# Matmuls of ones around the first transposes, and GpSimd in written order, at the beginning of a two-layer encoder kernel

## The chip, the cores and the metric

The kernel runs on one core of a Trainium2 chip. The metric is the device time of one execution in microseconds (us), shown as the median of several runs. The core has five engines with instruction queues of their own, which wait for each other through semaphores: TensorE (PE; its weight loads are shown apart as PEld), VectorE (DVE), ScalarE (ACT), GpSimd (POOL) and SyncE (SP), which here only issues DMAs. Matmuls write to PSUM, the accumulation memory; the other operands lie in SBUF.

## The reference

Two interleaved layers over 1024 tokens of width 1024, float32. Each layer is `x = x + mixer(rms_norm(x))`, then `x = x + ffn(rms_norm(x))`; a last `rms_norm` ends it.

- Layer 0 mixes with differential attention: 8 heads, each with two query/key pairs of 64, of which 16 are rotated by position, and values of 128. The weights of one softmax minus lambda times those of the other multiply the values; the result is normalised per head and projected.
- Layer 1 mixes with latent attention: 16 heads whose queries, keys and values come out of normalised low-rank projections (ranks 384 and 256) and a rotated key shared by the heads.
- The feed-forward part projects to 2 x 2816, applies a causal convolution of width 3, a gated SiLU, and projects back.

Attention is causal in chunks of 64 tokens.

## The kernel before, in words

Every float32 product is made of three matmuls in the faster type fp32r: an operand is split into a rounded part ("high", a cast, L127) and the rest ("low", a subtraction, L130). `mm3` (L119 to L121) issues the three. So each operand is transposed where needed, cast, and subtracted before PE can use it.

The change lies in `diff_attention`, at the beginning of layer 0. There the 1024 tokens come in as eight tiles `x` of 128 tokens. For each tile ACT sums the squares (`squares`, L157), DVE and POOL make the root (L164 and L167, a power), DVE normalises (`norm`, L370), PE transposes the tile in two groups of four 128x128 blocks (`turn`, L378), ACT casts the high half of each group (`high`) and DVE subtracts the low half (`parts_low`, `low`). The first head's three weight tensors (`which` 0 queries, 1 keys, 2 values) are split likewise (`w_high`, `w_low`). `piece(which, part)` then issues 24 matmuls, 256 tokens wide, that make a quarter of the tokens of one projection; `complete` rotates the result (`rope`: DVE L237 and L238, POOL L239 and L240) and splits it again (L574, L575 for keys; casts L127 on ACT and subtractions L130 on POOL for queries; a copy L560 for values, which are transposed later at L186).

Three things set the order of the work. From `region.__enter__()` to `region.__exit__()` the engines named there follow the order in which the code is written: PE, DVE and ACT. All else is placed by a planner that simulates the program and chooses which instruction each engine issues next; it also places every instruction after the region. Each queue is then executed in that order. POOL and SP are the planner's from the start.

After the region, `steps` runs the attention of head after head, four steps each. `prepare` fetches and splits the next head's weights (`fetch_w`, `split_w`: a cast on ACT, a subtraction on POOL); `units` issues the next projections, `scores` the query-key products (L1553 and L1554 in the first attention, mm3 into tiles named S in the second), `weigh`, `turn` and `product` what follows. The scores lie in two PSUM buffers named S; projections use one buffer named u, transposes and others three named b. The second attention, of layer 1, has the same kind of steps (exponential L1637, products with the values L1657 and L1658), all placed by the planner.

`ones` is a 128x128 tile of ones in fp32r (L208), made from the identity `ident`. `h4` is a piece of SBUF which the first attention uses only late in each head (`R.fin`).

Of the kernel before, what the change touches and what calls it, by code (L numbers as in the profile page):

```python
# [11 lines left out]
F32R = mybir.dt.float32r  # L12
AF = mybir.ActivationFunctionType
ALU = mybir.AluOpType
# [4 lines left out]
P = 128  # L19
# [7 lines left out]
DA_HEADS = 8  # L27
# [29 lines left out]
class Trunk:  # L57
# [123 lines left out]
    def turn_blocks(self, src, dst):  # L181
# [6 lines left out]
        self.hi(dst(0), v)  # L188
        self.lo(dst(1), v, dst(0))

    def gain(self, place, src):
        g = self.at(place, [P, src.shape[-1]])
        self.nc.sync.dma_start(g, src.partition_broadcast(P))
        return g


    def constants(self):
        nc, a = self.nc, self.a
        c = lambda name, shape, dt=F32: self.const.tile(shape, dt, name=name, tag=name)
        self.ident = c("ident", [P, P])  # L200
        make_identity(nc, self.ident)
        nc.scalar.preload_act_table_set("natural_log_exp_and_others")
        self.mhalf = c("mhalf", [P, 1])
        nc.gpsimd.memset(self.mhalf, -0.5)
        self.eps = c("eps", [P, 1])
        nc.gpsimd.memset(self.eps, EPS)
        self.ones = c("ones", [P, P], F32R)
        nc.vector.tensor_scalar(self.ones, self.ident, 0.0, 1.0, ALU.mult, ALU.add)  # L208
        self.conv = [c(f"conv{l}", [P, 2 * NF, 4]) for l in range(2)]
        self.g_sub = c("g_sub", [P, 1])  # L210
        self.neglam = c("neglam", [P, 1])
# [103 lines left out]
    def diff_attention(self, o_d, prefetch):  # L315
        nc, a = self.nc, self.a
# [7 lines left out]
            P=self.ring("u8", "u9", "u10", "u11", "u12"), pT=self.ring("u13", "u14", "u15"),  # L324
# [9 lines left out]
        raws = {}  # L334

        def fetch_w(h, which):
            if h < DA_HEADS:
                raws[h, which] = self.fetch(a["da_wqkv"][h, which], D)

        def split_w(h, which):  # L340
            if h < DA_HEADS:
                raw = raws.pop((h, which))
                w = self.w([P, 2, D], F32R)
                self.hi(w[:, 0, :], raw)
                self.lo(w[:, 1, :], raw, w[:, 0, :], nc.gpsimd)
                heads[h]["w", which] = w[:, 0, :], w[:, 1, :]

        def unit(h, which, half):
# [9 lines left out]
        def fetch_x(i):  # L358
            x.append(R.P([P, D]))
            nc.sync.dma_start(x[i], a["x"][i * P : (i + 1) * P, :])  # L360
# [5 lines left out]
        def squares(i):  # L366
            r[i] = self.squares(x[i], junk)
# [4 lines left out]
        def root(i):  # L372
            r[i] = self.root(r[i], D)

        def turn(i, kg):
            ps = part_of[i, kg] = self.bank()
            for k in range(4):
                nc.tensor.transpose(ps[:, k * P : (k + 1) * P], x[i][:, (4 * kg + k) * P : (4 * kg + k + 1) * P], self.ident)  # L378

        def parts(i, kg):  # L380
            s = slice((i % 4) * P, (i % 4 + 1) * P)
            return part_of[i, kg].rearrange("p (k s) -> p k s", s=P), [H[part][i // 4][kg][:, :, s] for part in range(2)]

        def high(i):
            for kg in range(2):
                src, (hi, lo) = parts(i, kg)
                self.hi(hi, src)
# [10 lines left out]
        def w_high(which):  # L398
            raw = raws[0, which]
            w = heads[0]["wt", which] = self.w([P, 2, D], F32R)  # L400
            heads[0]["w", which] = w[:, 0, :], w[:, 1, :]
            self.hi(w[:, 0, :], raw)

        def w_low(which):
            w = heads[0]["wt", which]
            self.lo(w[:, 1, :], raws.pop((0, which)), w[:, 0, :])
# [13 lines left out]
        def complete(which):  # L420
            return self.da_complete(R, accs[which], which, 0, heads[0], tab)

        def turns(i):
            for kg in range(2):
                turn(i, kg)
# [9 lines left out]
        nc.sync.dma_start(raws[0, 2], a["da_wqkv"][0, 2])  # L435
        fetch_tab(0)
        fetch_x(4)
        region = self.tc.manual_schedule(engines={mybir.EngineType.PE, mybir.EngineType.DVE, mybir.EngineType.Activation})
        region.__enter__()
        one, two = range(0, 4), range(4, 8)  # L440
        squares(0)
        root(0)
        norm(0)
        squares(1)
        root(1)
        turns(0)
        high(0)
        w_high(1)
        parts_low(0, 0)
# [1 line left out]
        parts_low(0, 1)  # L451
        squares(2)
        turns(1)
        high(1)
        w_low(1)
        root(2)
# [47 lines left out]
        queries, value = [complete(0)], [complete(2)]  # L504
# [8 lines left out]
        self.run(queries)  # L513
        fetch_w(1, 1)
        self.load_constants()
        region.__exit__(None, None, None)
        self.run(value)

        def prepare(t):
            h, p = divmod(t, 4)  # L520
            if p == 0:
                split_w(h + 1, 1)
                fetch_w(h + 1, 0)
            if p == 1:
                split_w(h + 1, 0)
                fetch_w(h + 1, 2)
            if p == 2:
                split_w(h + 1, 2)
            if p == 3:
                fetch_w(h + 2, 1)  # L530
            if h + 1 == DA_HEADS:
                prefetch()
# [732 lines left out]
    def mla_input(self, W, hts, turns, v_d, heads_of):  # L1265
# [28 lines left out]
        def latents(i):  # L1294
            acc = self.big()
            for k in range(KD):
                for b, m, kind in ((0, 384, "q"), (512, 288, "kv")):
                    wh, wl = where[kind, k]
                    self.mm3(acc[:, b : b + m], hts[i][:, 0, k, :], hts[i][:, 1, k, :], wh, wl, k == 0, k == KD - 1)
            nat = nats([P, 672])  # L1300
            for b, m, off, gain in ((0, 384, 0, g[0]), (512, 256, 384, g[1])):
                d = nat[:, off : off + m]
                r = self.rstd(acc[:, b : b + m], d, m)
                nc.vector.scalar_tensor_tensor(d, acc[:, b : b + m], r, gain, ALU.mult, ALU.mult)
            nc.scalar.copy(nat[:, 640:672], acc[:, 768:800])
            return nat
# [646 lines left out]
```

## Time and profile before

| what | us |
|---|---|
| median of 3 runs | 2432.36 (2431.1 to 2434.21) |
| the profiled execution | 2430.82 |
| its span, from first to last instruction | 2429.0 |
| TensorE busy | 2361.7 (97%) |
| DVE / ACT / POOL busy | 1899.3 / 1304.4 / 625.3 |

The page's rows of an engine's timeline show start and length in us, engine, line, what was done, output and input tile (buffer numbers left out) with their shapes, and in brackets how long the engine was idle before it and who ended that. A table of stretches shows, for each stretch of time, its length, then the busy time of PE, PEld, DVE, ACT and POOL with the number of instructions, the clock that TensorE was granted (1.00 is full), the share of the DMA engines, and GB/s. A row of waits shows who waited for whom, the total in us, how often, and the longest. Matmuls overlap each other, so their spacing, not their length, tells the rate.

### The profile page before, as it was taken

The numbers are of one execution on the slowest core, as the hardware profiler recorded it, in microseconds if no ns is written. First come the engines' busy times: TensorE is split into PE (matmuls) and PEld (weight loads), VectorE is DVE, ScalarE is ACT, GpSimd is POOL, SyncE is SP. The second block draws the span as 40 slices with busy tenths as digits, with TensorE's granted clock in tenths as the row PEclk, the third lists the DMA queues.
The fourth block names the chain that finished last, engine by engine and source line by source line (L and its number), as shares of the span: only waits on it lengthen the run. The fifth ranks groups of instructions, "written<-read, shape, count | busy, mean of one in ns | idle before, by whom it ended". The sixth has DMA issues, their size and how long they took to land. (4 is left out here: it accounts for less than half of the span.)

```text
span 2429.0 us, 32810 instructions
## 1 busy us (share of the span) xinstructions
PE 2361.7 (97%) x12032; PEld 2007.0 (83%) x12032; DVE 1899.3 (78%) x3094; ACT 1304.4 (54%) x2434; POOL 625.3 (26%) x500
## 2 busy tenths in 40 slices
PE   7999999999999999999999999999999999999998
PEld 6888878788888888878898788988888888887886
DVE  6677777756888888899964788886478888888997
ACT  5677776844444444444445777775344444444444
POOL 4545555425000000000042666664330000000001
PEclk9999999999999999999999999999999999999999
DMA  4111111333222222553221211123322222227502
GB/s 161 47 37 36 35 36 44 100 100 126 70 78 83 83 80 93 194 175 120 84 90 55 68 40 40 40 76 119 108 70 87 78 88 86 78 87 277 171 3 79
DMA packets 95793, 213.93 MB, mean 88 GB/s; under 512 B 8720, under 2 KB 33936, under 8 KB 95632
## 3 DMA queue, kind: packets, MB, share of 16 engines
q1 hardware_dynamic: 86448, 184.04, 22.9%
q10 hardware_dynamic: 9184, 27.79, 3.1%
q8 instruction: 95, 1.56, 0.3%
q14 instruction: 66, 0.54, 0.1%
HBM read 159.37 MB, written 52.43 MB: 87 GB/s over the span
## 5 line engine op out<-in xcount | busy, mean ns | idle before, releaser
L167 POOL TENSOR_TENSOR st<-st,mhalf 128x1 f32<-128x1 f32 x56 | 35.7, 638 | 1311.7 <-DVE st L164 1306.7
L127 ACT CAST u<-h 128x512 fp32r<-128x512 f32 (+2 forms) x242 | 146.1, 619 | 280.2 <-DVE h L779 260.1
L119 PE MATMUL S<-s,u 128*128 128x512 f32 (+1 forms) x752 | 286.0, 380 | 0.7 <-DVE s L130 0.5
L120 PE MATMUL S<-s,u 128*128 128x512 f32 (+1 forms) x752 | 284.6, 379 | 0.0
L121 PE MATMUL S<-s,u 128*128 128x512 f32 (+1 forms) x752 | 284.6, 378 | 0.0
L119 PE MATMUL b<-s,u 128*128 128x512 f32 x588 | 230.8, 392 | 2.1 <-DVE S L1635 1.0
L121 PE MATMUL b<-s,u 128*128 128x512 f32 x588 | 229.2, 390 | 0.0
L120 PE MATMUL b<-s,u 128*128 128x512 f32 x588 | 229.2, 390 | 0.0
L836 DVE SCALAR_TENSOR_TENSOR u<-u,conv,u 128x1023 f32<-128x1023 f32 (+1 forms) x176 | 224.7, 1277 | 1.6 <-ACT u L832 1.6
L149 POOL TENSOR_TENSOR u<-u,st 128x384 f32<-128x384 f32 (+7 forms) x160 | 169.2, 1067 | 151.4 <-DVE st L1643 107.8
L127 ACT CAST s<-u 128x512 fp32r<-128x512 f32 (+2 forms) x202 | 128.8, 673 | 110.4 <-PE u L121 35.9
L119 PE MATMUL u<-s,s 128*128 128x512 f32 (+1 forms) x440 | 176.7, 402 | 11.1 <-DVE h L238 4.5
L130 DVE TENSOR_TENSOR u<-b,u 128x512 fp32r<-128x512 f32 (+1 forms) x256 | 157.7, 629 | 24.3 <-ACT u L127 22.4
L121 PE MATMUL u<-s,s 128*128 128x512 f32 (+1 forms) x440 | 172.9, 393 | 0.0
L120 PE MATMUL u<-s,s 128*128 128x512 f32 (+1 forms) x440 | 172.2, 391 | 0.0
L119 PEld LDWEIGHTS S<-s,u 128*128 128x128 f32 x752 | 141.8, 189 | 27.9 <-DVE s L130 0.9
L121 PEld LDWEIGHTS S<-s,u 128*128 128x128 f32 x752 | 141.9, 189 | 26.2
L120 PEld LDWEIGHTS S<-s,u 128*128 128x128 f32 x752 | 141.9, 189 | 26.0
L127 ACT CAST u<-b 128x512 fp32r<-128x512 f32 (+1 forms) x256 | 133.5, 549 | 28.1 <-PE b L252 22.3
L839 ACT ACTIVATE u<-u 128x1024 f32<-128x1024 f32 x44 | 46.8, 1062 | 187.5 <-DVE u L836 187.5
L130 DVE TENSOR_TENSOR s<-u,s 128x512 fp32r<-128x512 f32 (+2 forms) x187 | 127.4, 714 | 17.7 <-ACT s L127 17.6
L130 DVE TENSOR_TENSOR u<-h,u 128x512 fp32r<-128x512 f32 x166 | 114.1, 687 | 32.4 <-ACT u L127 31.5
(263 smaller groups left out, 6632.1 us busy)
## 6 DMA issues: line engine op xcount, KB each, us to landing
u<-in_ffn_up SPq DMA_DIRECT2D x88, 512.0 KB, 3.9
g_d<-u ACTq DMA_DIRECT2D x44, 512.0 KB, 2.6
u<-in_ffn_down SPq DMA_DIRECT2D x66, 256.0 KB, 4.7
u<-g_d SPq DMA_DIRECT2D x62, 256.0 KB, 4.3
s<-in_da_wqkv SPq DMA_DIRECT2D x23, 512.0 KB, 3.3
x_d<-u SPq DMA_DIRECT2D x16, 512.0 KB, 3.0
s<-x_d SPq DMA_DIRECT2D x8, 1024.0 KB, 10.5
u<-o_d SPq DMA_DIRECT2D x24, 256.0 KB, 2.9
```

Of the source, the lines that this page charges most:

```text
L119: mm(out, lh, rl, start=first, stop=False, skip_group_check=onto)
L120: mm(out, lh, rh, start=False, stop=False, skip_group_check=onto)
L121: mm(out, ll, rh, start=False, stop=last, skip_group_check=onto)
L127: self.nc.scalar.copy(out, src)
L130: (eng or self.nc.vector).tensor_sub(out, src, hi.bitcast(F32))
L149: self.nc.gpsimd.tensor_mul(x, x, s.to_broadcast(list(x.shape)))
L167: nc.gpsimd.tensor_tensor(r, s, self.mhalf, ALU.pow)
L836: nc.vector.scalar_tensor_tensor(t[half][:, back:], u[half][:, : S - back], w, t[half][:, back:], ALU.mult, ALU.add)
L839: nc.scalar.activation(t[0], t[0], AF.Silu)
```

## The change

- A method `spin(n)` issues `n` matmuls of the ones tile with a 512-wide tile of ones into the u buffer. Nobody reads the results; the first piece writes the same buffer afterwards. `spin(14)` stands ahead of everything in the region, `spin(3)` after the first tile's transposes, `spin(1)` after the second tile's.
- The wide tile of ones is made by four DVE writes out of `ident`, in `h4`.
- POOL is added to the engines whose order in the region is the written one.
- The value's completion (`self.run(value)`) moves into the region, and the second head's key weights (1, 1) are split there, at its end, with the subtraction on DVE; `prepare` skips them then, since `raws` no longer has them.

```diff
+    def spin(self, n):
+        ps = self.bank("u")
+        for _ in range(n):
+            self.nc.tensor.matmul(ps, self.ones, self.wide, start=True, stop=True)
...
+        self.wide = self.at("h4", [P, 512], F32R)
+        for j in range(4):
+            nc.vector.tensor_scalar(self.wide[:, j * P : (j + 1) * P], self.ident, 0.0, 1.0, ALU.mult, ALU.add)
...
-        def split_w(h, which):
-            if h < DA_HEADS:
+        def split_w(h, which, eng=None):
+            if (h, which) in raws:
...
-                self.lo(w[:, 1, :], raw, w[:, 0, :], nc.gpsimd)
+                self.lo(w[:, 1, :], raw, w[:, 0, :], eng or nc.gpsimd)
...
-        region = self.tc.manual_schedule(engines={mybir.EngineType.PE, mybir.EngineType.DVE, mybir.EngineType.Activation})
+        region = self.tc.manual_schedule(engines={mybir.EngineType.PE, mybir.EngineType.DVE, mybir.EngineType.Activation, mybir.EngineType.Pool})
...
+        self.spin(14)
         squares(0)
...
         turns(0)
+        self.spin(3)
         high(0)
...
         turns(1)
+        self.spin(1)
         high(1)
...
         fetch_w(1, 1)
         self.load_constants()
+        self.run(value)
+        split_w(1, 1, nc.vector)
         region.__exit__(None, None, None)
-        self.run(value)
```

As built, each engine has the same instructions as before but for the 18 matmuls, the four writes and the subtraction that goes from POOL to DVE. Their order is the same outside the beginning, save in the second attention, where the planner places PE's, DVE's, ACT's and POOL's instructions differently.

## The prediction

> **What bounds the kernel now.** I read the page's totals first, then a table of stretches, then the timeline of each engine over the first 66 us, then PE's waits.
>
> ```profile
> span 2429.0 us, 32810 instructions
> PE 2361.7 (97%) x12032; PEld 2007.0 (83%) x12032; DVE 1899.3 (78%) x3094; ACT 1304.4 (54%) x2434; POOL 625.3 (26%) x500
> ...
> 14.20:19.40 5.20, 5.15 (x24) 5.15 (x25) 4.45 (x5) 2.12 (x4) 1.46 (x1) 1.00 0.91 334
> 36.40:51.30 14.90, 11.10 (x64) 8.95 (x62) 11.78 (x21) 7.98 (x14) 12.18 (x8) 1.00 0.11 37
> 75.00:105.00 30.00, 30.00 (x153) 25.07 (x152) 18.50 (x33) 19.44 (x37) 12.79 (x10) 1.00 0.05 18
> ```
>
> TensorE is busy 97% of the span. From 75 to 105 us it never rests, so whatever the beginning saves or loses ahead of that arrives at the end unless a later stall takes it up. Two stretches of the beginning are slow in different ways. From 14.2 to 19.4 us PE is full (5.15 of 5.20) with only 24 matmuls; from 36.4 to 51.3 it idles 3.8 of 14.9 us. The profiled execution took 2430.82 us, 1.8 more than its span; the median of the runs, 2432.36, is 1.5 above it. The sums below are made on the profiled one, and their difference is put on the median.
>
> ```profile
> 1.98 0.52 DVE L208 TENSOR_SCALAR ones<-ident 128x128 fp32r<-128x128 f32 x1 [1.98 <-POOL ident masks.py:199]
> 5.79 0.15 DVE L164 TENSOR_SCALAR st<-st 128x1 f32<-128x1 f32 x1 [3.29 <-ACT u L157]
> 8.03 1.97 PE L378 MATMUL b<-ident,u 128*128 128x128 f32 x8 [8.03 <-DVE u L370]
> 9.18 0.59 ACT L127 CAST s<-b 128x512 fp32r<-128x512 f32 x1 [0.20 <-PE b L378]
> 9.80 0.69 DVE L130 TENSOR_TENSOR s<-b,s 128x512 fp32r<-128x512 f32 x1 [0.63 <-ACT s L127]
> 11.73 1.97 PE L378 MATMUL b<-ident,u 128*128 128x128 f32 x8 [1.74 <-DVE u L370]
> 12.20 1.21 DVE L130 TENSOR_TENSOR s<-s,s 128x1024 fp32r<-128x1024 f32 x1
> 14.25 0.58 PE L119 MATMUL u<-s,s 128*128 128x256 f32 x1 [0.55 <-DVE s L130]
> 14.63 0.42 PE L120 MATMUL u<-s,s 128*128 128x256 f32 x1
> 19.11 0.42 PE L120 MATMUL u<-s,s 128*128 128x256 f32 x1
> 19.52 1.04 PE L378 MATMUL b<-ident,u 128*128 128x128 f32 x8
> 20.52 0.28 PE L120 MATMUL S<-s,s 128*128 128x256 f32 x1
> 23.03 0.28 PE L120 MATMUL S<-s,s 128*128 128x256 f32 x1
> 66.83 0.39 PE L119 MATMUL u<-s,s 128*128 128x512 f32 x1
> 70.92 0.39 PE L119 MATMUL u<-s,s 128*128 128x512 f32 x1
> ```
>
> These are timeline rows (start, length, engine, line, tiles, idle before it and who ended that). The 2nd and 23rd matmul of the first projection piece start 4.48 us apart, 0.213 each; in the next piece, of the same shape, 2.51, 0.120 each. Eight transposes take 1.97 us twice and then 1.04. So TensorE runs at half speed up to about 19.4 us. At full speed a 512-wide matmul takes (70.92 - 66.83) / 18 = 0.227.
>
> **The change part by part.** *The tile of ones.* Four more writes on DVE, of the form of the 0.52 us row, which is DVE's first; the small DVE rows (0.15) bound them from below. They end between 3.1 and 4.6 us, I take 4.0, inside DVE's idle 3.29 us: free.
>
> *Fourteen wide matmuls.* They wait for that tile alone and start at 4.0. At half speed each takes 2 x 0.213 = 0.427, all of them 6.0, ending at 10.0. The closed state lasted 3.4 us where the trace shows it whole (below); opened after 3.4 us, eight run slow and six fast, 3.4 + 1.4, ending at 8.8. I take 9.3 (bounds 7.9 to 10.6 with the start's own). The first transposes could start at 8.03, so they now wait for the filler, 1.3 us, but then take 1.04. Their first half, which ACT's cast waits for, is ready at about 9.8 against 9.18: 0.6 late. DVE runs from 9.80 without a wait into the pieces' low halves, so norm, second transposes and the first piece move by that 0.6, to 14.85 (14.1 to 16.1).
>
> *Three and one wide matmuls.* 0.7 and 0.23 us, in PE's waits of 1.74 and 0.55 ahead of the second transposes and the first piece. The second transposes shorten by 0.93, which covers the last. Nothing on the path.
>
> *The first piece at full speed.* 24 x (0.213 - 0.120) = 2.25 less. With the late start it ends 1.65 earlier. How much passes on is DVE's matter:
>
> ```profile
> 18.07 1.28 DVE L370 SCALAR_TENSOR_TENSOR u<-u,st,s 128x1024 f32<-128x1024 f32 x1 [0.44 <-POOL st L167]
> 20.78 1.29 DVE L130 TENSOR_TENSOR s<-b,s 128x512 fp32r<-128x512 f32 x2 [1.42 <-ACT s L127]
> ```
>
> The third tile's low halves cannot start before the norm ahead of them on DVE ends (19.35), so at most 1.43 of it passes. I take 1.3 gained; ends: 1.4 gained with an early filler, and 0.6 lost (up to 1.9) where the piece stays slow.
>
> *GpSimd in written order, the weight split taken from it.*
>
> ```profile
> 38.38 1.05 ACT L127 CAST s<-s 128x1024 fp32r<-128x1024 f32 x1 [1.84 <-DVE u L370]
> 39.50 2.40 POOL L130 TENSOR_TENSOR s<-s,s 128x1024 fp32r<-128x1024 f32 x1
> 41.84 1.30 POOL L239 TENSOR_TENSOR h<-h,s 128x512 f32<-128x512 f32 x1
> 42.01 3.38 DVE L575 SCALAR_TENSOR_TENSOR u<-h,u 64x512 fp32r<-64x512 f32 x2
> 43.22 1.62 POOL L240 TENSOR_TENSOR h<-h,h 128x512 f32<-128x512 f32 x1
> 45.48 0.59 ACT L560 COPY h<-S 128x512 f32<-128x512 f32 x1 [3.91 <-DVE u L575]
> 46.09 2.54 ACT L127 CAST u<-h 64x512 fp32r<-64x512 f32 x4
> 46.78 2.62 POOL L130 TENSOR_TENSOR h<-h,u 64x512 fp32r<-64x512 f32 x2 [1.95 <-ACT u L127]
> 48.11 0.33 PE L1553 MATMUL S<-u,h 128*128 128x128 f32 x1 [0.49 <-POOL h L130]
> 49.45 0.33 PE L1553 MATMUL S<-u,h 128*128 128x128 f32 x1 [0.63 <-POOL h L130]
> 51.34 0.50 PE L119 MATMUL u<-s,s 128*128 128x512 f32 x1 [1.16 <-DVE h L238]
> 52.61 0.37 ACT L1568 ACTIVATE u<-S,st 128x128 f32<-128x128 f32 x1 [2.33 <-DVE st L1562]
> 56.52 1.41 DVE L575 SCALAR_TENSOR_TENSOR u<-h,u 64x512 fp32r<-64x512 f32 x2
> ```
>
> Today POOL splits the second head's weights (2.40) between the rotations of keys and queries. Without it the query's rotation begins when DVE's shuffle is done, some 1.6 us earlier, and ends about 43.2 instead of 44.84. DVE's L575 takes 3.38 beside POOL and 1.41 alone; with POOL out of its second half it ends near 44.3 instead of 45.39. ACT's copy waits for L575, its four casts follow, then POOL's low halves of the queries, and for those PE waits 0.49 and 0.63, and then 1.16 for DVE. All move by 1.1. Ends: nothing, if L575 keeps its 3.38; 2.28, the three waits together. I take 1.1. The split itself now costs DVE 1.21 and ACT 1.05. Both are placed where DVE waits for scores and ACT waits 2.33: nothing; without that cover up to 1.2 on the first softmax, with an L575 behind it on DVE. On SP one x tile goes ahead of a weight fetch, and that order has no wait on a DMA behind it: nothing.
>
> *The planner.* POOL enters the hand-written region, so what the planner makes of later stages can change. Matched one by one, 1,643 of the 12,034 earlier matmuls stand at another place, all but five of them in the second attention, by their count the stretch from 1361 to 1652 us, up to 31 places away. The work is the same.
>
> ```profile
> 1361.00:1652.00 291.00, 286.77 (x1869) 257.85 (x1868) 237.30 (x578) 220.03 (x484) 192.79 (x154) 1.00 0.16 49
> PE S L119 <- ACT u L1637: 0.8, 3, 0.4
> ```
>
> These are the stretch in the table of stretches (PE, PEld, DVE, ACT, POOL busy) and one row of PE's waits in it (total, times, longest). PE idles 4.2 us there; no more can be won. What can be lost has no such bound. I take nothing, with ends of 4.2 gained and the price below lost.
>
> *Sum:* -1.3 - 1.1 = -2.4: 2428.4 for an execution like the profiled one, 2430.0 as median.
>
> **The rivals.** *The clock closes again before the first piece.* Between the filler and the piece PE has two idle stretches of over 1 us around transposes.
>
> ```profile
> 594.74 0.63 PE L186 MATMUL b<-ident,h 128*128 128x128 f32 x4 [3.52 <-DVE h L638]
> ...
> 596.00:596.40 0.40, 0.40 (x4) 0.40 (x5) 0.37 (x1) 0.40 (x1) 0.00 (x0) 0.93 0.00 0
> 599.60:600.00 0.40, 0.40 (x5) 0.40 (x4) 0.10 (x1) 0.27 (x1) 0.40 (x1) 0.80 0.00 0
> ```
>
> The first row is from PE's timeline, the others from the table of stretches, where the granted clock is the third column from the end. It falls near 596.4, after 3.52 idle and some 1.6 us of work that is mostly transposes, and is back near 599.7: the 3.4 used above. In the new start the waits are shorter but lie close together, with one 0.23 us matmul among transposes. If the clock falls there, the piece stays slow and only the filler's delay is left: +0.6 - 1.1 = -0.5, 2431.9. For it: transposes did not hold the clock up at 596. Against it: no single gap reaches 3.5. [...]
>
> *The new order of the second attention fills PE's idle time:* it takes back 3.5 of the 4.2 us, 2426.5. For it: scores are issued up to 28 places earlier at its start. Against: those waits are scattered.
>
> *The same order is slower.* PE works in order and scores need one of two PSUM buffers; pulled ahead or pushed back, a group stands until ACT's exponential frees it, and all behind it stands too. The trace has three such waits, up to 0.4. Of 114 groups 18 more at 0.4 cost 7.2 and carry the time over 2437.2, the 0.2% bound; 30 make 12: 2442. Against: PE, DVE and ACT have spare time there (4, 54 and 71 of 291 us).
>
> **How the numbers follow.** Forecast 0.45, closed clock 0.25, filled idle time 0.18, slower order 0.12. A change of 0.2% (4.9 us) is about what a measurement of this kernel can tell from none. Faster by that: the filled order, and the best ends of the forecast, 0.20; slower 0.10; same 0.70. The range runs from below the filled case, 2425, to 2437, leaving out 0.1 on either side. Alone, the forecast's own ends give 2428.7 (1.4 and 2.3 gained) to 2432 (filler at 10.6, the piece still fast, nothing from POOL: 0.4 gained).
>
> **What would show it.** Right: transposes of 1.04 from the start, a first piece near 0.120 a matmul ending before 18 us, L575 under 3 us, the waits before 51 us gone, PE at the 75 us stage about 2.4 us earlier. Wrong: 0.213 in the piece, a filler that ends after 10.6, or second-attention waits that sum beyond 7 us.

## The result and the profile after

| | before | after |
|---|---|---|
| median of 19 runs each, us | 2432.36 (2426.7 to 2436.68) | 2438.08 (2433.31 to 2444.58) |
| the profiled execution, us | 2430.82 | 2441.52 |
| its span, us | 2429.0 | 2439.7 |

The ratio of the medians is 1.0024, with a 95% interval of 1.0016 to 1.0032: slower by 5.7 us, where 2.4 faster was forecast. The time lies above the range, 2425 to 2437. The profiled execution of after is 3.4 above its median and that of before 1.5 below, so the traces show about twice the difference of the medians. Sizes of parts are read from the traces, verdicts from the medians.

The totals of after's page:

```profile
span 2439.7 us, 32823 instructions
PE 2373.5 (97%) x12050; PEld 2012.9 (83%) x12050; DVE 1901.2 (78%) x3099; ACT 1304.0 (53%) x2434; POOL 624.4 (26%) x499
```

They say little: the shares are those of before. To find the place I set the start of each matmul of after (its 18 new ones left out) against that of the same matmul of before. This table is worked out from all matmul rows of the two timelines; below, "matmul 400" is the one with 400 ahead of it:

| matmuls ahead of it | before, us | after minus before, us |
|---|---|---|
| 0 | 8.0 | +1.29 |
| 200 | 40.0 | -1.58 |
| 400 | 83.6 | -1.24 |
| 2,600 | 506.6 | -1.32 |
| 4,000 | 797.7 | -3.64 |
| 6,600 | 1354.5 | -2.46 |
| 7,000 | 1422.1 | -4.72 |
| 8,600 | 1667.0 | +7.27 |
| 12,031 (the last) | 2419.2 | +10.7 |

The beginning saves 1.2 us and keeps it for 500 us. From 506 to 1354 us PE's instructions stand in the same order, and yet after gains 2.3 us more by 798 us. Most of that is one wait. In before DVE stands for a DMA at 590.82, runs late and beside GpSimd, and PE waits 3.52 us behind it (the row at 594.74 in the prediction); in after DVE does not stand for the DMA, and PE waits 1.77:

```profile
590.82 2.11 DVE L661 SCALAR_TENSOR_TENSOR u<-u,st,u 128x1024 f32<-128x1024 f32 x1 [1.60 <-DMA x_d<-u]
```

```profile
587.91 1.28 DVE L674 SCALAR_TENSOR_TENSOR u<-u,st,u 128x1024 f32<-128x1024 f32 x1 [0.67 <-POOL st L167]
591.01 0.63 PE L186 MATMUL b<-ident,h 128*128 128x128 f32 x4 [1.77 <-DVE h L651]
```

The prediction does not have this gain; the experiments and the last section come back to it. Short falls of the clock, to a granted 0.50 for 3.4 us each, came at 596 and 1354 us in before and at 592, 1033 and 1350 in after; the one at 1033 goes with the 1.2 us that after loses again by 1354. The order is new in the second attention: it gains 2.3 us at first, and then loses 12.0 in 1,600 matmuls. The rest of the loss, 3.4 us after matmul 8,600, is again in the same order; after's clock falls at 1773, 1790 and 2244 us, before's only at 1767, the very end aside. The last of these steps, 2.3 us near 2244, is more than such a fall can cost (1.7, half of 3.4): PE also waits 1.94 us there, 0.88 in before.

**The second attention.** Tables of stretches, before and then after (length, then busy time of PE, PEld, DVE, ACT and POOL with their counts, granted clock, DMA share, GB/s):

```profile
1440.00:1500.00 60.00, 60.00 (x398) 54.39 (x397) 49.93 (x124) 46.35 (x102) 41.77 (x33) 1.00 0.14 40
1500.00:1560.00 60.00, 59.73 (x396) 54.10 (x395) 48.82 (x121) 46.92 (x103) 41.05 (x32) 1.00 0.14 41
```

```profile
1440.00:1500.00 60.00, 57.89 (x373) 51.66 (x372) 47.56 (x117) 42.86 (x97) 38.59 (x31) 1.00 0.14 40
1500.00:1560.00 60.00, 58.45 (x376) 51.75 (x375) 47.15 (x116) 44.40 (x96) 40.23 (x31) 1.00 0.15 41
```

Before issues 398 and 396 matmuls in 60 us with hardly an idle moment; after 373 and 376, and PE idles 2.1 and 1.6 us. The clock is full in all four. After's waits of PE from 1361 to 1665 us (who waits for whom: total us, times, longest):

```profile
PE b L261 <- DVE u L130: 5.0, 10, 0.9
PE S L119 <- ACT u L1650: 1.9, 2, 1.7
PE b L261 <- DVE S L1648: 1.2, 1, 1.2
```

The first row is new in size; before has for the same pair, over a stretch of the same work:

```profile
PE b L252 <- DVE u L130: 1.7, 3, 0.7
```

What happens there stands in after's timeline of PE and DVE:

```profile
1443.89 1.25 PE L261 MATMUL b<-ident,u 128*128 128x128 f32 x10
1444.02 0.96 DVE L1649 TENSOR_REDUCE st<-S 128x1 f32<-128x768 f32 x1
1445.20 0.56 DVE L1649 TENSOR_REDUCE st<-S 128x1 f32<-128x384 f32 x1
1445.28 0.28 PE L1671 MATMUL u<-u,s 128*128 128x128 f32 x1
1445.67 1.28 DVE L130 TENSOR_TENSOR u<-b,u 128x512 fp32r<-128x512 f32 x2
1446.41 0.55 PE L261 MATMUL b<-ident,u 128*128 128x128 f32 x3 [0.85 <-DVE u L130]
...
1490.13 0.55 PE L261 MATMUL b<-ident,u 128*128 128x128 f32 x3 [0.86 <-DVE u L130]
```

PE issues ten transposes in a row into the b buffers, then four products, and wants a b buffer for the next three transposes at 1445.56. DVE empties a buffer with the low half L130, but reduces two score rows first and gets to it at 1445.67. PE stands until 1446.41. In before's order the low halves lie between the reductions, and nothing waits:

```profile
1444.54 0.53 DVE L130 TENSOR_TENSOR u<-b,u 128x384 fp32r<-128x384 f32 x1
1445.00 0.93 DVE L1636 TENSOR_REDUCE st<-S 128x1 f32<-128x768 f32 x1
1445.86 0.54 DVE L130 TENSOR_TENSOR u<-b,u 128x384 fp32r<-128x384 f32 x1
...
1447.09 0.42 PE L119 MATMUL S<-s,s 128*128 128x384 f32 x1
...
1488.62 0.42 PE L119 MATMUL S<-s,s 128*128 128x384 f32 x1
```

The last two rows are the same place one pair of heads (272 matmuls) apart: 41.53 us. After's two waits are 43.72 us apart, and the wait comes again at 1533.86 and 1577.59, each time a pair later. So the new order is not a mishap or two but a longer cycle, 2.2 us a pair. Of the 12.0 us that are lost between matmul 7,000 and 8,600, PE's idle time grows by 6.6 (2.4 to 9.0); a fall of the clock at 1623.1, 3.4 us long, costs up to 1.7. The rest, about 3.7, I did not resolve. That fall may belong to the order: the kernel with the single matmul alone (below) has one at 1625.5, behind a wait of 1.84 for ACT where after has 1.70, and no other profile has a fall between 1400 and 1700 us.

**The beginning.** After's timeline, which answers to the rows of before in the prediction:

```profile
3.77 5.71 PE L195 MATMUL u<-h,ones 128*128 128x512 f32 x14 [3.77 <-DVE h L217]
9.31 1.03 PE L387 MATMUL b<-ident,u 128*128 128x128 f32 x8
9.95 1.07 ACT L127 CAST s<-b 128x512 fp32r<-128x512 f32 x2 [0.90 <-PE b L387]
13.35 0.48 PE L195 MATMUL u<-h,ones 128*128 128x512 f32 x1
14.99 0.36 PE L119 MATMUL u<-s,s 128*128 128x256 f32 x1 [1.16 <-DVE s L130]
15.19 0.28 PE L120 MATMUL u<-s,s 128*128 128x256 f32 x1
17.70 0.28 PE L120 MATMUL u<-s,s 128*128 128x256 f32 x1
17.95 1.03 PE L387 MATMUL b<-ident,u 128*128 128x128 f32 x8
40.41 2.22 DVE L588 SCALAR_TENSOR_TENSOR u<-h,u 64x512 fp32r<-64x512 f32 x2
48.20 0.50 PE L119 MATMUL u<-s,s 128*128 128x512 f32 x1 [0.74 <-DVE h L247]
48.95 2.41 POOL L130 TENSOR_TENSOR s<-s,s 128x1024 fp32r<-128x1024 f32 x1
49.89 2.54 DVE L130 TENSOR_TENSOR s<-s,s 128x1024 fp32r<-128x1024 f32 x1
51.31 2.26 POOL L249 TENSOR_TENSOR h<-h,h 128x512 f32<-128x512 f32 x1
53.97 0.69 DVE L1594 SCALAR_TENSOR_TENSOR u<-u,st 128x128 f32<-128x128 f32 x1 [1.40 <-POOL u L149]
57.07 1.05 ACT L127 CAST s<-s 128x1024 fp32r<-128x1024 f32 x1 [1.57 <-DMA s<-in_da_wqkv]
64.75 0.50 PE L119 MATMUL u<-s,s 128*128 128x512 f32 x1 [2.73 <-DVE h L247]
```

The piece runs at (17.70 - 15.19) / 21 = 0.120 a matmul, and the transposes behind it start at 17.95 instead of 19.52. The spacing shows the speed here, not the clock column: before's trace has its first record of the clock at 19.5 us, and up to there the column reads 1.00. The projection at 48.20 stood at 51.34 before: 3.14 earlier, 1.6 from the faster piece and 1.5 from GpSimd's order. By 53.97 only 0.66 is left of it (before 54.63).

### The profile page after: what moved, and what is told of

It is laid out like the page before. It is cut to its first block, busy times and chain, and to the rows that moved or that the text cites. A ratio compares the mean times of both kernels' runs of the same rounds, so it can differ in the third digit from the quotient of the medians.

```text
span 2439.7 us, 32823 instructions
## 1 busy us (share of the span) xinstructions
PE 2373.5 (97%) x12050; PEld 2012.9 (83%) x12050; DVE 1901.2 (78%) x3099; ACT 1304.0 (53%) x2434; POOL 624.4 (26%) x499
## 3 DMA queue, kind: packets, MB, share of 16 engines
HBM read 159.37 MB, written 52.43 MB: 87 GB/s over the span
## 4 chain that ended last, share of the span: by engine, by line
PE 82%; DVE 7%; ACT 4%; DMA 2%; issue 2%; POOL 2%; SPq 0%; ACTq 0%; POOLq 0%; DVEq 0%
PE S L119 13%; PE S L121 13%; PE S L120 13%; PE b L119 8%; PE b L121 8%; PE b L120 8%; PE u L119 4%; PE u L120 4%; PE u L121 3%; PE b L261 2%; PE u L1671 1%; PE u L1670 1%; DVE s L130 1%; PE b L186 1%; DMA u<-g_d 1%
## 5 line engine op out<-in xcount | busy, mean ns | idle before, releaser
L149 POOL TENSOR_TENSOR u<-u,st 128x384 f32<-128x384 f32 (+7 forms) x160 | 169.2, 1065 | 152.7 <-DVE st L1656 109.5
L130 DVE TENSOR_TENSOR u<-b,u 128x512 fp32r<-128x512 f32 (+1 forms) x256 | 158.0, 631 | 27.4 <-ACT u L127 25.3
L261 PE MATMUL b<-ident,u 128*128 128x128 f32 x864 | 137.2, 276 | 8.5 <-DVE u L130 6.1
L130 DVE TENSOR_TENSOR s<-u,s 128x512 fp32r<-128x512 f32 (+2 forms) x187 | 127.5, 714 | 18.7 <-ACT s L127 18.6
```

Source lines behind the costliest of these rows:

```text
L130: (eng or self.nc.vector).tensor_sub(out, src, hi.bitcast(F32))
L149: self.nc.gpsimd.tensor_mul(x, x, s.to_broadcast(list(x.shape)))
L261: self.nc.tensor.transpose(ps[:, j * P : (j + 1) * P], probs[t][:, k : k + P], self.ident)
```

## The experiments

A ratio below comes from the rounds in which both kernels ran, and can differ by up to 0.08% from that of the two medians beside it. GpSimd in the region was not run by itself: as built, that alone changes no engine's order.

**One filler matmul less.** From after, the last of the 18 goes. As built, the second attention then has before's order. My theory by then: the order is the loss; the rival: the beginning is.

```diff
         turns(1)
-        self.spin(1)
         high(1)
```

> The changed kernel without the single wide matmul after the second tile's transposes; the 14 and the 3 stay, and so do the split and GpSimd in the region. As built, TensorE's and ACT's order in the second attention is then the one of before. Theory A (the planner's new order in the second attention costs 7 to 10 us, the beginning gains 1 to 1.6): 2431 us, 1.3 below before; the second attention takes within 1 us of its time before. Theory B (the loss comes with the filler matmuls themselves, through the clock or through TensorE's work, not with the order): 2437 to 2438, as the changed kernel, since 17 of 18 matmuls are still there.

2432.57 against 2433.89: 0.9993, 0.9984 to 1.0002. The loss is gone with one matmul of 0.2 us; matmul 8,600 stands +1.8 and not +7.3.

**That matmul alone.** Before, with the tile of ones and only `spin(1)` after the second tile's transposes: no other filler, no split, GpSimd left to the planner. As built, every engine has after's order from the middle of the program on.

```diff
         turns(1)
+        self.spin(1)
         high(1)
```

> The kernel before with the wide tile of ones and only the single matmul after the second tile's transposes: no 14, no 3, no split, GpSimd not in the region. As built, the beginning has the old order, and from the middle on every engine has the order of the changed kernel. Theory A: 7 to 10 us slower than before, 2439 to 2442, all of it between 1361 and 1680 us, with the beginning unchanged. Theory B: one matmul of 0.4 us in an idle time of TensorE: 2432.4, no change.

2438.71 against 2433.89: 1.0023, 1.0014 to 1.0032. The whole loss, without the rest of the change. Its waits of PE in the second attention are after's:

```profile
PE b L261 <- DVE u L130: 5.0, 10, 0.9
PE S L119 <- ACT u L1647: 2.0, 2, 1.8
PE b L261 <- DVE S L1645: 1.2, 1, 1.2
```

Matmul 6,600 stands +0.1 and matmul 8,600 +10.4. More falls of the clock do not explain it: at a granted clock of 0.995 its runs take 2441.5 on the mean (3 runs) and before's 2433.7 (13 runs), at 0.996 2438.6 (4) and 2433.1 (10). The two runs together show that the order of the second attention makes the slowdown, and that the rest of the change at the beginning is not needed for it.

**The split and GpSimd's order alone.** After without filler and without the tile.

```diff
-        self.spin(14)
...
-        self.spin(3)
...
-        self.spin(1)
```

> The split of the second head's weights at the end of the region with its subtraction on DVE, the value inside the region, GpSimd in the region; no filler and no tile of ones. The planner's order in the second attention is as before but for some ten matmuls. My prediction's term: 1.1 us gained, 2431.3. What the changed kernel's trace suggests: the gain is there at the first scores (about 1.5) and is taken back by 65 us, where DVE's subtraction runs 2.54 us beside GpSimd's next split: 2432 to 2433, no change.

2434.01 against 2433.89: 1.0001, 0.9992 to 1.001. No gain is seen of the part forecast at -1.1, though the interval still holds that much; in the trace matmul 400 starts 0.7 later than before's. That trace also has a fall of the clock near 50 us, which before's lacks, so where the gain went is read from after's.

**Another count of filler, everything else kept.** As built, 16 for 14 also brings before's order back.

```diff
-        self.spin(14)
+        self.spin(16)
```

> The changed kernel with 16 in place of 14 matmuls ahead of the first transposes, the single one kept. As built, the second attention has the order of before. Theory A: the order decides, not the number of matmuls: 2431 to 2432 (two more fast matmuls delay the first transposes by about 0.45). Theory B: slower than the changed kernel, 2438.5 or more.

2432.2 against 2433.89: 0.9992, 0.9983 to 1.0. Two filler matmuls more, and by the ratios 0.3% faster than after: the count of filler matters by the order that the planner makes of it, not by its length.

**Filler without the split.** Before with the tile, `spin(14)` and `spin(3)`; no single, no split, GpSimd left to the planner; before's order in the second attention. It was run twice, the second time beside the run with the weights fetched apart (below).

```diff
+        self.spin(14)
         squares(0)
...
         turns(0)
+        self.spin(3)
```

> The kernel before with the wide tile, the 14 and the 3 matmuls; no single one, no split, GpSimd not in the region. The second attention keeps the order of before. If the filler alone carries the gain: 2431 to 2432, about 1.5 below before, more where the clock stays up through the first piece than where it falls near 14 us, as it did in the profiles of e1 and e4. If the split carried a part of e1's gain: less than e1's, about no change.

> e5 once more (filler 14 and 3 alone), beside e9 on the same chip: 0.998 of before if e5's 2429.4 holds.

2429.38 against 2433.24, 0.9978 (0.9969 to 0.9987), and 2429.69 against 2433.79, 0.9985 (0.9976 to 0.9994): faster than both kernels. In the traces the start of matmul 400 is only 0.7 earlier, or not at all, while the medians differ by about 4 us; so the faster beginning is the smaller part of them. Most of the gain lies at 594 us: between matmul 2,600 and 4,000 each of the two profiles gains 3.6. PE's wait there is 1.77 and 1.76 instead of 3.52, as in after, and the clock, which falls behind it in before, does not fall. All seven profiles with 14 or 16 fillers ahead have the short wait (1.75 to 1.77), the other five the long one (3.51 or 3.52); five of the seven have no fall of the clock there, and all of the other five have one. The prediction and the expectations do not speak of this; that the filler is worth 4 us is luck. The rows can't be summed up to the medians: before's profiled execution is itself below its median, and the falls later on lie elsewhere in each execution.

**Does the clock hold?** As the last, with six fillers between the transposes instead of three.

```diff
-        self.spin(3)
+        self.spin(6)
```

> As e5, with 6 matmuls in place of the 3: the idle time of TensorE between the first and the second transposes is filled (1.5 us in the changed kernel). [...]

2430.37 against 2433.24: 0.9982, 0.9974 to 0.9991. That is no less than with three fillers (0.9978). The forecast's rival of a closed clock is read from the profiles of these kernels. One row of the tables of stretches of the first run with fillers 14 and 3 alone, and one of the run with 16:

```profile
15.20:15.60 0.40, 0.40 (x4) 0.40 (x4) 0.40 (x2) 0.40 (x1) 0.00 (x0) 0.50 0.98 384
```

```profile
14.40:14.80 0.40, 0.00 (x0) 0.00 (x0) 0.40 (x1) 0.40 (x1) 0.40 (x1) 0.62 1.15 435
```

After has 1.00 in these stretches, and so has the run with six:

```profile
15.60:16.00 0.40, 0.40 (x4) 0.40 (x5) 0.40 (x2) 0.40 (x2) 0.00 (x0) 1.00 0.94 364
```

So the closed clock did come, in the profiles of three of the seven kernels and repeats with long filler (without the single, with 16, and 14 and 3 the first time), not in after's, and not when 14 and 3 were run again. With six it held, in one profile, but so it did with three the second time; the six are not shown to be what held it. Where it closed, the medians do not show it: they are of other executions.

**The split earlier.** From the split alone, with `split_w` ahead of `load_constants`, so that DVE would subtract while it has nothing else to do.

```diff
         fetch_w(1, 1)
+        split_w(1, 1, nc.vector)
         self.load_constants()
         self.run(value)
-        split_w(1, 1, nc.vector)
```

> e3 with the split one step earlier: ahead of the constants' sums in place of behind the value, so that ACT's cast and DVE's subtraction fall into their waits near 40 and 46 us, where GpSimd is idle; no filler. If the gain of GpSimd's freed queue is taken back in e3 because DVE's subtraction runs 2.5 us beside GpSimd's next split and holds up the first softmax: the subtraction takes 1.2 to 1.4, and TensorE is 1 us or more ahead of e3 at 85 us; time 2432 to 2433. If it is taken back by something else (the fetch of the next weights, GpSimd's own next split): as e3 at 85 us.

A miss: 2436.45 against 2433.24, 1.0008 (1.0 to 1.0017), and matmul 400 starts 3.2 later than before's, where the split alone has 0.7. Its timeline and its waits of PE in the first 85 us:

```profile
48.19 1.23 DVE L130 TENSOR_TENSOR s<-s,s 128x1024 fp32r<-128x1024 f32 x1 [4.35 <-ACT s L127]
49.23 2.38 POOL L130 TENSOR_TENSOR s<-s,s 128x1024 fp32r<-128x1024 f32 x1 [1.36 <-issue]
49.39 2.30 DVE L229 TENSOR_TENSOR h<-h 128x64 f32<-128x64 f32 x1
```

```profile
PE u L119 <- DVE h L244: 5.4, 2, 4.3
```

DVE waits 4.35 for ACT's cast, which stands behind the queries' casts in the written order, and the constants' sums and the rotation stand behind it on DVE. I had looked at when DVE is free, not at when its operand is.

**A third order.** Before with `spin(4)` and `spin(1)` around the second transposes. As built, PE's order in the second attention differs from both, for some 610 matmuls of its first half, and is before's afterwards.

```diff
         turns(0)
+        self.spin(4)
...
         turns(1)
+        self.spin(1)
```

> The kernel before with the wide tile, four wide matmuls after the first tile's transposes and one after the second's, none ahead. As built, the planner gives a third order: TensorE's differs from before's only in the first part of the second attention, for some 610 matmuls, and is before's again from there. Theory A (each order has its price in the stretch where it differs, as the other new order costs 2.2 us for each pair of heads): the time differs from before only by what that stretch shows, anything between 2 gained (what the changed kernel gained ahead of its steady part) and 5 lost; with the beginning's small gain. Theory that any departure from before's order is slow: 2435 or more.

2433.47 against 2433.24: 0.9997, 0.9988 to 1.0006. Matmul 400 starts 2.6 earlier, the best beginning of all, with nothing ahead of the first transposes. Its stretches from 1440 us on show the rest (before's stand above):

```profile
1440.00:1500.00 60.00, 58.30 (x374) 51.62 (x373) 47.85 (x120) 42.48 (x97) 39.28 (x32) 1.00 0.14 40
1500.00:1560.00 60.00, 59.73 (x396) 54.07 (x395) 48.86 (x121) 47.34 (x104) 41.39 (x33) 1.00 0.14 41
```

Where the order is new it makes 374 matmuls in 60 us, as after does; where it is before's again, 396. It loses mainly while the order differs, and that takes back the beginning's gain: matmul 8,600 stands -0.3.

**The weights fetched apart.** After without the single, the second head's key weights in a piece of SBUF of their own instead of the buffer that the next fetch needs. It asks which of two things takes the split's gain back: the late DMA, or DVE beside GpSimd.

```diff
-        self.spin(1)
...
-        fetch_w(1, 1)
+        raws[1, 1] = self.at("u13", [P, D])
+        nc.sync.dma_start(raws[1, 1], a["da_wqkv"][1, 1])
```

> e1 (filler 14 and 3, split on DVE, GpSimd in the region) with the second head's key weights fetched into another piece of SBUF (u13, not used before the second step of the attention) instead of one of the two raw buffers. In the changed kernel and in e1 the next weight fetch leaves only near 52 us, when DVE's moved subtraction has read the raw buffer, against 41.9 before; ACT's cast waits for it with the exponentials behind it, and TensorE waits 2.7 us where it waited 1.1. If that is how the split costs time: the fetch leaves near 42, ACT's wait of 1.5 us for the DMA is gone, TensorE's longest wait there is below 1.5 us, and the time is 1.5 to 3 us below e1's 2432.6, at e5's 2429 to 2431. If DVE's subtraction itself holds up the softmax: the wait stays near 2.7 and the time is e1's.

2428.79 against 2433.79: 0.9987, 0.9978 to 0.9995. The fetch that ACT waits for left at 19.85, earlier than the expected 42, and ACT's wait for the DMA (1.57 in after) is gone. But PE's wait shrank only from 2.7 to 2.4, for DVE's subtraction is as slow as in after (its timeline and its waits):

```profile
48.98 2.40 POOL L130 TENSOR_TENSOR s<-s,s 128x1024 fp32r<-128x1024 f32 x1
49.93 2.53 DVE L130 TENSOR_TENSOR s<-u,s 128x1024 fp32r<-128x1024 f32 x1
```

```profile
PE u L119 <- DVE h L247: 3.1, 2, 2.4
```

By these rows the subtraction beside GpSimd is what holds the first softmax up, and the DMA a small part. Between matmul 200 and 400 this kernel gains 0.1 and after loses 0.3; the filler alone gains 0.4 in its first profile and loses 1.2 in its second, whose clock falls at 50.6 us. Whether the split is better left out altogether can't be told: the intervals of this kernel, of the one without the single and of the filler alone overlap.

## Why the prediction was wrong

**The planner** (taken at nothing) is the step that failed, and it alone makes the sign. The text named the 1,643 moved matmuls and wrote "the work is the same", and that what can be lost has no bound, and then took zero. The runs show +0.23% for the order alone, 5.6 us by that ratio and 4.8 by the two medians. The time that came is that of the third rival, the same order slower, which had 0.12. But that rival's price was made from another wait: scores that stand for ACT's exponential, 18 more at 0.4. Those grew from 0.8 to 1.9 us. What grew more was a transpose that waits for DVE's low half, which the prediction did not speak of, and it came back in each pair of heads. The argument against the rival, that PE, DVE and ACT have 4, 54 and 71 us to spare in the stretch, was beside the point: DVE still had its spare time, but did two things in the wrong order for PE. The sign by which the text would know itself wrong, waits in the second attention beyond 7 us, did come: 5.0 + 1.9 + 1.2 = 8.1.

**The filler and the first piece** (-1.3) came out as forecast, in part by luck. The filler starts at 3.77 (4.0 forecast) and ends at the transposes' 9.31 (9.3); these take 1.03 (1.04); ACT's cast starts at 9.95 (9.8); the piece at 14.99 (14.85), at 0.120 a matmul. PE is 1.58 earlier at matmul 200, a little over the 1.43 that the text took for the most that could pass. But the 9.3 was the middle of two cases, and the clock opened in neither way: eleven of the fourteen ran slow, 0.43 apart up to 8.62, where the text had eight or all. The start 0.23 earlier than taken made up for some of that. A gain of the same size stood in no term at all, the wait at 594 us that came out 1.75 shorter. The tile's four writes lay in DVE's idle time as said.

**GpSimd and the split** (-1.1). The first half was right: L588 takes 2.22 instead of 3.38, the waits of 0.49 and 0.63 shrink to one of 0.23, and the projection at 48.20 has gained 1.5 beside the first piece's part. The second half failed: "Both are placed where DVE waits for scores and ACT waits 2.33: nothing". DVE's subtraction was to take 1.21 and took 2.54, beside GpSimd's split of other weights (48.95 to 51.36); GpSimd's rotation step behind it, 1.29 in before, took 2.26; its scaling (L149) came late, DVE waited 1.40 for it, and PE 2.73 at 64.75 where before's longest wait of that kind was 1.2. "That order has no wait on a DMA behind it" failed too, though by another route than the one it speaks of: the next fetch needs the buffer which the split reads, left at 52.46 instead of 41.92, and ACT waited 1.57 for it. Net: 1.0001 alone (0.9992 to 1.001). The number 1.2 for a lost cover stood in the text as the price if the cover is gone; what was missed is that beside GpSimd's part it doubles (1.21 to 2.54).

**The closed clock** (2431.9, 0.25) did not happen in after's profile, but it was no remote case: it came in three of seven profiles of its kind. In the kernel with fillers 14 and 3 the clock fell at 15.2 with no idle stretch over 1.5 us from the filler on; from 10.95, where the three fillers end, to the first piece at 14.81 PE had run eight transposes, 1.09 us, and nothing else. What part the transposes have in that, no run shows.

**The filled idle time** (2426.5, 0.18) is refuted for these orders: both new orders gain at the start of the second attention (2.3 us in after) and lose more in its steady part.

## What to carry to other kernels

Where a planner orders what follows, the smallest edit ahead of it can give another order of a stage that fills the bottleneck engine, and that order is the larger part of the risk: compare the orders as built, and price a moved order by what it repeats, once per pass of the stage's loop, not by a few single waits. Set the two traces against each other over the whole span: a gain or a loss can lie 500 us behind the edit, where nothing was changed. In a stage in which one engine is full, read for each of its buffers which instruction frees it and what stands ahead of that instruction on its own engine. An instruction moved into another engine's idle time can cost more than its length: DVE's subtraction, 1.21 alone, took 2.54 beside GpSimd's, and where its operand came late DVE stood 4.35 for it. Both are read from the neighbours' timelines.

## What the runs showed of the hardware

DVE's subtraction of two SBUF tiles ended only behind GpSimd's. In after it starts at 49.89, GpSimd's ends at 51.36 (48.95 + 2.41), and 1.07 later, at 52.43, DVE is done; alone, at 12.20 in before, it takes 1.21. GpSimd's next step, at 51.31, ends 1.14 behind that, at 53.57; in before, at 54.06, it takes 1.29. In the kernel with the early split a DVE instruction on 64 columns (L229 there; L223 in before, where it took 0.22) took 2.30, to 51.69, where GpSimd's subtraction ended at 51.61. So in these three cases the later instruction ended 0.08 to 1.14 behind the other engine's, by no more than its own length alone, as if it had stood until then; what holds it is not shown. Here such a step is to be priced at the durations of both together.

The clock fell near the first piece although no idle stretch from the filler on was longer than 1.5 us, at 15.2 in the kernel with 14 and 3, and at 14.5 in the one with 16. In after, whose single filler lies between the second transposes and the first piece, it stayed up, but so it did in the weights-apart kernel without one, whose first piece starts at 15.01. So the single does not decide it. What goes together in all seven profiles is when the clock had opened: where it fell, it had opened at 8.2, 7.7 and 8.4 us, and fell 6.8 us later; where it stayed up it had opened between 8.6 (after) and 10.0, and 6.8 us later, at 15.4 to 16.8, more of the first piece had run. Seven profiles do not prove that this decides it, and no run sets the moment of opening by itself.

The wait at 594 us hangs on one part of one DMA. In the five kernels without the long filler, fifteen of the sixteen parts of `x_d<-u` land within 2.7 us of the issue and the last 4.6 after it; in the seven with the filler all land within 2.7. In the five, the trace's DMA records have a 16 KB transfer of the kind "instruction" somewhere between 0.9 and 3.6 us after that issue; in the seven it ends at least 2.3 us ahead of the issue. My guess from this timing is that a fetch of instructions delays the late part, and that the filler, which makes the program longer, moves the fetch; the timing agrees in all twelve profiles, but no run was made to show it.
